# A rotation's sine product moved into the transposed-tile buffer, and VectorE's lane work placed behind the rotations already traced

## The chip, the core and the metric

The kernel runs on one NeuronCore of a Trainium2 chip. The metric is device time in microseconds (us) for one launch. PE is TensorE's matrix multiply, VectorE and ScalarE are the two elementwise engines, GpSimd a third one, and SP is the queue of SyncE, which issues nearly all transfers (DMAs) of this kernel. Each engine takes its own queue of instructions in order; semaphores make one wait for another.

## What is computed

One decoder layer over 2048 positions of width 1024 in fp32: adaptive RMS norm, one wide projection, two recurrent mixers side by side (HGRN2 and retention), their gated sum, an output projection, a last norm. The change lies in the retention half and in the order of the work beside it:

```python
proj = h @ w_in        # split: hq hf hi hz | rq rk rv rz | ga gb
qB = rotary(rq); kB = rotary(rk)          # per head: [t1*cos - t2*sin, t1*sin + t2*cos]
scores = einsum('bhnid,bhnjd->bhnij', qc, kc) * Dm
oB = scores @ vc + (qc * xi) @ R_prev     # R = gamma^C * R + (kc*zeta)^T vc, over chunks of 128
S_t = diag(f_t) S_{t-1} + (1 - f_t) i_t^T ; o_t = S_t^T q_t      # HGRN2
m = sigmoid(ga) * (norm(oA) * silu(hz)) + sigmoid(gb) * (norm(oB) * silu(rz))
out = rms_norm(x + gate * (m @ w_out))
```

## The kernel before

**Tiling.** The 2048 positions are two halves (`sb` 0 and 1) of eight chunks of 128 (`c`; chunk numbers run 0 to 15 in tile names). The eight heads are four pairs `p`. For each half and pair, `do_pair` runs four projections with weights streamed in from HBM: `a` (HGRN2's f and q, tiles gf and gq), `c` (values, gv), `b` (retention's q and k, gr; only for p = 0 and p = 2, each for two pairs) and `d` (the gates, gg, once per head). A projection of one chunk is 8 steps (`kt`) of 3 matmuls of 128x512: each fp32 operand is a high and a low fp32r part, and `mm3` adds hi*hi, hi*lo and lo*hi. Accumulators are PSUM tiles `pd`, three of them in rotation, so a projection's chunk can start when the chunk three before it has been read out.

**Weights.** `Ring` holds nine (hi, lo) weight tiles. When PE has used a tile for the last time (in the last chunk of a projection, step by step), `release` lets the next be split: ScalarE copies the high part (L468, wha to whd), VectorE subtracts for the low part (L469, wla to wld). The raw weights come by DMA on SP (L456).

**Rotations.** There are four groups of eight rotations, at (sb 0, p 0), (sb 0, p 2), (sb 1, p 0), (sb 1, p 2): the first, second, third and fourth group below. `rotate` reads one gr accumulator on VectorE: product with the cosine into `qk` (L754, two buffers), product with the sine into `qs` (L754, one buffer), a subtraction (L762) and an addition (L763) that make the turned q and k in `qk`, a 32x32 block transposition of `qk` into `tr` (L766, two buffers), and the zeta-weighted k into `kz` (L768, two buffers). Then `send` posts five DMAs on SP (L779, L783) that write `tr` and `kz` to DRAM. The accumulator is free when both products are done.

**Lanes.** Beside the projections run "lanes": `tree` (HGRN2's decay products), `hgrn_out` (HGRN2's outputs, tiles poh, and the states st) and `retention`. Each projection step ticks a counter in `Background`; every 9 ticks `burst` traces one more piece of each lane. For chunk 0 `hgrn_out` issues the poh matmuls on PE, a copy of the new state (st, L729) or its update (L731) on VectorE, then sums of squares on ScalarE (L681), a power on GpSimd (L115) and the scaling into v on VectorE (L684). In the second half the states are first scaled (L697). `retention` fetches turned k and q for a chunk by DMAs on SP (qpad L803, kpad L804, kT L807), then PE makes the scores (rt), VectorE weights them (scm, L824), and PE makes por.

**Order.** PE keeps program order. The other engines' queues are ordered by a scheduler from its own estimates of readiness, within the dependencies; buffers of a tag are reused in turn, and a write into a reused buffer waits for its last reader (for `tr`: the four DMAs that send it). `tc.issue_after(ins)` adds, to each instruction traced inside its block on the engine of `ins`, the edge that it stands behind `ins`. The last two chunks of a gr projection (6 and 7, or 14 and 15) are computed together, step by step (`group_two`), and the pair's lanes start just before them, so that PE's queue holds poh and the first rt among the steps of gr_6, gr_7 and the first gg.

Of the kernel before, what the change touches and what calls it, by code (L numbers as in the profile page):

```python
# [9 lines left out]
F32 = mybir.dt.float32  # L10
# [12 lines left out]
P = 128  # L23
# [18 lines left out]
def tile_hybrid(ctx: ExitStack, tc: tile.TileContext, a: dict, out: bass.AP):  # L42
    nc = tc.nc
    V, S, G = nc.vector, nc.scalar, nc.gpsimd

    class InOrder:

        def __init__(self):
            self.on = False
# [14 lines left out]
    upool = ctx.enter_context(tc.tile_pool(name="upool", bufs=1))  # L64
# [9 lines left out]
    def small_ps(name, tag):  # L74
        return pp.tile([P, 512], F32, name=name, tag=tag, bufs=small[tag])
# [100 lines left out]
    def ada_row(j):  # L176

        acc = upool.tile([P, 512], F32, name=f"acc{j}", tag="qk", bufs=2)
        bg_ = upool.tile([P, 512], F32, name=f"gate{j}", tag="tr", bufs=2)
        nc.sync.dma_start(out=bg_, in_=a["bgate"][:, j * 512 : (j + 1) * 512].broadcast_to([P, 512]))  # L180
        for k2 in range(KT // 2):
            w = wpool.tile([P, 2, 512], F32, name=f"wg{j}_{k2}", tag="raw", bufs=NRAW)
            nc.sync.dma_start(out=w, in_=a["w_gate"][j, 2 * k2 : 2 * k2 + 2].rearrange("k p n -> p k n"))
            for i in range(2):
                kt = 2 * k2 + i
                if kt == 0:
                    V.tensor_scalar(out=acc, in0=w[:, i, :], scalar1=sc[:, 0:1], scalar2=None, op0=ALU.mult)
                else:
                    V.scalar_tensor_tensor(
                        out=acc, in0=w[:, i, :], scalar=sc[:, kt : kt + 1], in1=acc, op0=ALU.mult, op1=ALU.add  # L190
                    )
            yield
        ps = small_ps(f"gps{j}", "sc")
        PE.matmul(out=ps, lhsT=ones, rhs=acc, start=True, stop=True)
        V.tensor_tensor(out=bg_, in0=ps, in1=bg_, op=ALU.add)
        gate[j] = bg_

    gate = {}
# [13 lines left out]
    for i in range(NQP):  # L212
        t = cpool.tile([P, 256], F32, name=f"qpad{i}", tag=f"qpad{i}")
# [5 lines left out]
    for i in range(NQP):  # L219
        t = cpool.tile([P, 256], F32, name=f"kpad{i}", tag=f"kpad{i}")  # L220
# [9 lines left out]
    class Background:  # L230

        def __init__(self):
            self.lanes = []
            self.side = []
            self.late = []
            self.since = 0.0
            self.beat = 0.0
            self.bursts = 0
            self.now = 0.0
            self.posts = []  # L240

        def burst(self):
            self.bursts += 1
            done, now = False, list(self.lanes)
            while now:
                again = []
                for g in now:
                    try:
                        said = next(g)
                    except StopIteration:  # L250
                        self.lanes.remove(g)
                        done = True
                        continue
                    done = done or said is not True
                    if said == "mid":
                        again.append(g)
                now = again
            self.merges()
            return done
# [48 lines left out]
    bg = Background()  # L308
# [27 lines left out]
    def x_rstd(t, xt, nm):  # L336
        sq = upool.tile([P, 512], F32, name=f"sq{nm}", tag="sg", bufs=3)
        ss = upool.tile([P, 2], F32, name=f"xss{nm}", tag="ss", bufs=4)
        for i in range(2):
            S.activation(out=sq, in_=xt[i], func=AF.Square, accum_out=ss[:, i : i + 1])  # L340
        r = upool.tile([P, 2], F32, name=f"xr{nm}", tag="rr", bufs=4)
        V.tensor_tensor(out=r[:, 0:1], in0=ss[:, 0:1], in1=ss[:, 1:2], op=ALU.add)
        rstd_of(r[:, 0:1], r[:, 0:1], 1, D)
        return r[:, 0:1]
# [38 lines left out]
    def block_r(b):  # L383

        rb = upool.tile([P, 512], F32, name=f"rb{b}", tag="qk", bufs=2)
        for t in range(4):
            xt = []
            for i in range(2):
                xt.append(upool.tile([P, 512], F32, name=f"xt{b}_{t}_{i}", tag="tr", bufs=2))
                nc.sync.dma_start(out=xt[i], in_=a["x"][(4 * b + t) * P : (4 * b + t + 1) * P, i * 512 : (i + 1) * 512])  # L390
            yield
            yield
            r = x_rstd(t, xt, f"b{b}_{t}")
            dg = upool.tile([P, P], F32, name=f"dgr{b}_{t}", tag="jk", bufs=1)
            G.tensor_scalar(out=dg, in0=ident, scalar1=r, scalar2=None, op0=ALU.mult)
            yield
            yield
            ps = small_ps(f"rb{b}_{t}", "sc")
            PE.matmul(out=ps[:, 0:P], lhsT=ones, rhs=dg, start=True, stop=True)
            S.activation(out=rb[:, t * P : (t + 1) * P], in_=ps[:, 0:P], func=AF.Copy)  # L400
        rbs[b] = rb
# [343 lines left out]
    turned_qk, rot = {}, {}  # L745

    def rotate(p, gc, ps):

        nm = f"{p}_{gc}"
        qk = upool.tile([P, 512], F32, name=f"qk{nm}", tag="qk", bufs=2)  # L750
        qs = upool.tile([P, 512], F32, name=f"qs{nm}", tag="qs", bufs=1)
        pv = ps.rearrange("p (g d) -> p g d", d=32)
        for dst, tab in ((qk, rot["cos"]), (qs, rot["sin"])):
            V.tensor_tensor(  # L754
                out=dst.rearrange("p (g d) -> p g d", d=32),
                in0=pv,
                in1=tab[:, gc % CH * 32 : (gc % CH + 1) * 32].unsqueeze(1).broadcast_to([P, 16, 32]),
                op=ALU.mult,
            )
        qkv = qk.rearrange("p (g two d) -> p g two d", two=2, d=32)  # L760
        qsv = qs.rearrange("p (g two d) -> p g two d", two=2, d=32)
        V.tensor_tensor(out=qkv[:, :, 0, :], in0=qkv[:, :, 0, :], in1=qsv[:, :, 1, :], op=ALU.subtract)  # L762
        V.tensor_tensor(out=qkv[:, :, 1, :], in0=qkv[:, :, 1, :], in1=qsv[:, :, 0, :], op=ALU.add)  # L763

        tr = upool.tile([P, 512], F32, name=f"tr{nm}", tag="tr", bufs=2)
        V.transpose(out=tr, in_=qk)  # L766
        kz = upool.tile([P, 256], F32, name=f"kz{nm}", tag="kz", bufs=2)
        V.tensor_tensor(  # L768
            out=kz.rearrange("p (w j d) -> p w j d", w=2, j=2),
            in0=qk.rearrange("p (w s j d) -> p w s j d", w=2, s=2, j=2)[:, :, 1],  # L770
            in1=zeta[:, 2 * p : 2 * p + 4].rearrange("p (w j) -> p w j", w=2).unsqueeze(3).broadcast_to([P, 2, 2, 64]),
            op=ALU.mult,
        )
        dm = dpool.tile([512, P], F32, name=f"qkT{nm}", tag="qkT", bufs=2 * CH)
        dz = dpool.tile([P, 256], F32, name=f"kz{nm}", tag="kzd", bufs=2 * CH)

        def send():
            for i in range(4):
                nc.sync.dma_start(  # L779
                    out=dm[:, 32 * i : 32 * i + 32].rearrange("(j a) t -> a j t", a=32),  # L780
                    in_=tr[32 * i : 32 * i + 32].rearrange("a (j t) -> a j t", t=32),
                )
            nc.sync.dma_start(out=dz, in_=kz)  # L783
            for w in range(2):
                turned_qk[p + w, gc] = (dm[256 * w : 256 * w + 256], dz[:, P * w : P * w + P])

        bg.post(4.0, send)
# [100 lines left out]
    def do_pair(sb, p, hook):  # L888
# [50 lines left out]
        if p % 2 == 0:  # L939
            for c, ps in group_toks(sb, ("b", sb, p), f"gr{p}", 0, start_lanes):  # L940
                rotate(p, sb * CH + c, ps)
# [157 lines left out]
    for j in range(2):  # L1099
        t = fgs[:, j * 512 : (j + 1) * 512]  # L1100
# [141 lines left out]
```

## Time and profile before

| | us |
|---|---|
| three runs: median (lowest to highest) | 2126.49 (2126.24 to 2127.15) |
| the profiled execution | 2124.74 |
| its span, first to last instruction | 2122.9 |
| PE busy, matmuls | 2053.1 |
| VectorE busy | 1097.3 |
| ScalarE busy | 572.3 |

The mean granted TensorE clock of the profiled execution is 0.989 of full speed. The page gives the busy time of each engine and the chain of work that ended last; the waits say for each instruction what ended the idle time before it; the timeline lists instructions by start and length; windows give busy times and the granted clock by stretch.

### The profile page before, as it was taken

Reading aid. Unit: us, or ns where it says so; the run is one execution under the profiler, and the core shown is the slowest. Engines: PE = TensorE matmul, PEld = TensorE weight load, DVE = VectorE, ACT = ScalarE, POOL = GpSimd, SP = SyncE. Lnnn points to the kernel's source line nnn. Section 1 sums busy time; section 2 is a strip of 40 time slices with the busy share of each in tenths; the row PEclk is TensorE's granted clock in tenths of the full one; section 3 lists DMA queues with packets and bytes.
Section 4 is the critical chain, followed back from the end, with each engine's and each line's share of the span. In section 5 each row is a group of like instructions: output and inputs, shape, how many; then the busy total and the mean of one; then the engine's idle time right before and its main releaser. Section 6 shows DMA issues by size and latency. Waiting matters only on the chain.

```text
span 2122.9 us, 38010 instructions
## 1 busy us (share of the span) xinstructions
PE 2053.1 (97%) x15320; PEld 1710.0 (81%) x15320; DVE 1097.3 (52%) x2441; ACT 572.3 (27%) x1389; POOL 139.8 (7%) x274
## 2 busy tenths in 40 slices
PE   6999999999997999999997999999997999999998
PEld 4887888888886888887886888888886888888886
DVE  7366544553455534557454544454454544567553
ACT  7212321332122221334221221332121221324221
POOL 1000100010001100121000100010000100010000
PEclk9999999999999999999999999999999999999999
DMA  8135221322144221434144221322144221346531
GB/s 310 41 74 128 63 65 41 91 60 57 41 103 107 78 55 41 105 109 141 41 103 94 69 63 41 84 65 58 41 103 105 70 61 41 84 142 191 175 133 60
DMA packets 322799, 187.65 MB, mean 88 GB/s; under 512 B 236096, under 2 KB 284736, under 8 KB 322624
## 3 DMA queue, kind: packets, MB, share of 16 engines
q1 hardware_dynamic: 322624, 185.23, 32.3%
q8 instruction: 120, 1.97, 0.4%
q14 instruction: 55, 0.45, 0.1%
HBM read 147.39 MB, written 37.75 MB: 87 GB/s over the span
## 4 chain that ended last, share of the span: by engine, by line
PE 91%; DVE 4%; DMA 2%; SPq 1%; issue 1%; POOL 1%; ACT 0%; DVEq 0%; POOLq 0%; ACTq 0%
PE gg L52 30%; PE gv L52 16%; PE gq L52 8%; PE ops L52 8%; PE gf L52 8%; PE gr L52 8%; PE poh L52 4%; PE por L52 4%; PE lv L52 3%; PE rt L52 1%; DVE wa L169 1%; DMA kT<-qkT 0%; DVE tr L766 0%; DMA k<-dk 0%; DVE h L358 0%
## 5 line engine op out<-in xcount | busy, mean ns | idle before, releaser
L52 PE MATMUL gg<-whd,h 128*128 128x512 f32 x2048 | 662.5, 396 | 4.6 <-DVE qs L754 4.6
L52 PEld LDWEIGHTS gg<-whd,h 128*128 128x128 f32 x2048 | 386.7, 189 | 84.7 <-issue 6.3
L52 PE MATMUL gg<-wld,h 128*128 128x512 f32 x1024 | 400.0, 391 | 1.5 <-DVE wld L469 1.5
L52 PE MATMUL gv<-whc,h 128*128 128x512 f32 x1024 | 331.5, 397 | 0.0
L52 PEld LDWEIGHTS gv<-whc,h 128*128 128x128 f32 x1024 | 193.1, 189 | 41.1 <-DVE h L358 0.4
L52 PEld LDWEIGHTS gg<-wld,h 128*128 128x128 f32 x1024 | 193.7, 189 | 39.4 <-DVE wld L469 1.9
L52 PE MATMUL gv<-wlc,h 128*128 128x512 f32 x512 | 199.2, 392 | 0.8 <-DVE wlc L469 0.8
L52 PE MATMUL gr<-whb,h 128*128 128x512 f32 x512 | 162.0, 392 | 0.0
L52 PE MATMUL gf<-h,wha 128*128 128x512 f32 x512 | 159.0, 390 | 2.1 <-DVE h L358 2.1
L52 PE MATMUL gq<-h,wha 128*128 128x512 f32 x512 | 157.7, 389 | 0.0
L52 PE MATMUL ops<-wo,mh 128*128 128x512 f32 x512 | 157.6, 389 | 0.0
L468 ACT ACTIVATE whd<-wd 128x512 fp32r<-128x512 f32 x128 | 78.1, 628 | 191.4 <-DMA wd<-in_w_d_dram 91.1
L612 DVE TENSOR_TENSOR q<-q,f 128x1024 f32<-128x1024 f32 x56 | 68.6, 1224 | 117.6 <-PE lv L52 117.6
L856 ACT ACTIVATE sgg<-gg 128x512 f32<-128x512 f32 x128 | 75.1, 596 | 172.9 <-PE gg L52 171.5
L469 DVE TENSOR_TENSOR wld<-wd,whd 128x512 fp32r<-128x512 f32 x128 | 85.7, 687 | 58.9 <-ACT whd L468 58.9
L52 PEld LDWEIGHTS gf<-h,wha 128*128 128x128 f32 x512 | 96.1, 188 | 24.1 <-DVE h L358 3.5
L115 POOL TENSOR_TENSOR rrr<-ssr,mhalf 128x2 f32<-128x2 f32 x64 | 44.8, 700 | 1039.7 <-DVE ssr L114 1039.7
L52 PEld LDWEIGHTS gv<-wlc,h 128*128 128x128 f32 x512 | 96.7, 189 | 20.4 <-DVE wlc L469 1.4
L52 PEld LDWEIGHTS gr<-whb,h 128*128 128x128 f32 x512 | 96.1, 188 | 20.0
L52 PEld LDWEIGHTS ops<-wo,mh 128*128 128x128 f32 x512 | 96.1, 188 | 20.0
L52 PEld LDWEIGHTS gq<-h,wha 128*128 128x128 f32 x512 | 96.0, 188 | 19.9
L681 ACT ACTIVATE jkr<-por 128x128 f32<-128x128 f32 x128 | 35.5, 277 | 242.6 <-DVE rs L843 201.8
(162 smaller groups left out, 2897.0 us busy)
## 6 DMA issues: line engine op xcount, KB each, us to landing
wd<-in_w_d_dram SPq DMA_DIRECT2D x64, 512.0 KB, 3.7
wc<-in_w_c_dram SPq DMA_DIRECT2D x32, 512.0 KB, 3.7
wa<-in_w_a_dram SPq DMA_DIRECT2D x32, 512.0 KB, 3.7
wa<-in_w_ada_dram SPq DMA_DIRECT2D x16, 512.0 KB, 8.3
wb<-in_w_b_dram SPq DMA_DIRECT2D x32, 256.0 KB, 3.2
qkT<-tr SPq DMA_DIRECT2D x128, 64.0 KB, 2.6
dk<-f SPq DMA_DIRECT2D x16, 512.0 KB, 2.8
k<-dk SPq DMA_DIRECT2D x64, 128.0 KB, 3.8
```

Of the source, the lines that this page charges most:

```text
L52: made = nc.tensor.matmul(**kw)
L115: G.tensor_tensor(out=dst, in0=ss, in1=mhalf.broadcast_to([P, width]), op=ALU.pow)
L169: V.tensor_tensor_reduce(out=w, in0=w, in1=scb, scale=1.0, scalar=bad[:, i * KT + kt : i * KT + kt + 1], op0=ALU.mult, op1=ALU.add, accum_ ...
L468: S.activation(out=hi, in_=w, func=AF.Copy)
L469: V.tensor_tensor(out=lo, in0=w, in1=hi, op=ALU.subtract)
L612: V.tensor_tensor(out=qv, in0=qv, in1=tv[:, :, :, 0:1].broadcast_to([P, NU, nb, m]), op=ALU.mult)
L681: S.activation(out=junk, in_=po[:, i * P : (i + 1) * P], func=AF.Square, accum_out=ss[:, i : i + 1])
L856: S.activation(out=sg, in_=ps, func=AF.Sigmoid)
```

## The change

`rotate` has no `qs` any more: the sine product is written into the `tr` buffer, from which subtraction and addition read it, and the transposition then overwrites it. `tr` has three buffers (also for the two other users of the tag, `ada_row` and `block_r`), `kz` has three. And `Background.burst` runs inside `issue_after` of the last rotation's kz product, so that VectorE's instructions of a burst stand behind the rotations that were traced before it.

```diff
+            self.hold = None
         def burst(self):
+            if self.hold is None:
+                return self.one_burst()
+            with tc.issue_after(self.hold):
+                return self.one_burst()
+        def one_burst(self):
...
-        qs = upool.tile([P, 512], F32, name=f"qs{nm}", tag="qs", bufs=1)
+        tr = upool.tile([P, 512], F32, name=f"tr{nm}", tag="tr", bufs=3)
         pv = ps.rearrange("p (g d) -> p g d", d=32)
-        for dst, tab in ((qk, rot["cos"]), (qs, rot["sin"])):
+        for dst, tab in ((qk, rot["cos"]), (tr, rot["sin"])):
...
-        qsv = qs.rearrange("p (g two d) -> p g two d", two=2, d=32)
+        qsv = tr.rearrange("p (g two d) -> p g two d", two=2, d=32)
...
-        tr = upool.tile([P, 512], F32, name=f"tr{nm}", tag="tr", bufs=2)
         V.transpose(out=tr, in_=qk)
-        kz = upool.tile([P, 256], F32, name=f"kz{nm}", tag="kz", bufs=2)
-        V.tensor_tensor(
+        kz = upool.tile([P, 256], F32, name=f"kz{nm}", tag="kz", bufs=3)
+        last = V.tensor_tensor(
             out=kz.rearrange("p (w j d) -> p w j d", w=2, j=2),
...
+        bg.hold = last.ins
```

In `ada_row` and `block_r` the diff only raises `bufs` of the tag `tr` from 2 to 3.

PE's queue holds the same rows in the same order as before. SP's queue differs only where `block_r` loads x between the halves, at a dozen of 765 rows, ScalarE's at 3 rows. What moves is VectorE's queue, in the four groups.

Second group (sb 0, p 2), VectorE before, from the last addition of rotation 4 on (the number behind the name is the chunk; st_129 and st_130 are the states of the two heads):

```order
L763 TENSOR_TENSOR qk_4_6085<-qk_4_6085,qs_4_6086 128x8x32
L729 COPY st_129<-poh_0_6151 128x128
L729 COPY st_130<-poh_0_6151 128x128
L469 TENSOR_TENSOR wld_6171<-wd_0_5778,whd_6170 128x512
L684 SCALAR_TENSOR_TENSOR v_0_5221<-poh_0_6151,rrh_0_6159,gn_2_0_6139 128x128 x2
L469 TENSOR_TENSOR wld_6183<-wd_1_5838,whd_6182 128x512
L469 TENSOR_TENSOR wld_6202<-wd_1_5838,whd_6201 128x512
L731 SCALAR_TENSOR_TENSOR st_129<-st_129,tl_0_5886,poh_1_6230 128x128
L731 SCALAR_TENSOR_TENSOR st_130<-st_130,tl_0_5886,poh_1_6230 128x128
L684 SCALAR_TENSOR_TENSOR v_1_5324<-poh_1_6230,rrh_1_6240,gn_2_0_6139 128x128 x2
L766 STREAM_TRANSPOSE tr_3_6049<-qk_3_6043 128x512
L768 TENSOR_TENSOR kz_3_6051<-qk_3_6043,zeta 128x256
```

The same place now, from the transposition of rotation 4 on:

```order
L773 STREAM_TRANSPOSE tr_4_6074<-qk_4_6073 128x512
L775 TENSOR_TENSOR kz_4_6080<-qk_4_6073,zeta 128x256
L477 TENSOR_TENSOR wld_6157<-wd_0_5770,whd_6156 128x512
L477 TENSOR_TENSOR wld_6169<-wd_1_5830,whd_6168 128x512
L477 TENSOR_TENSOR wld_6188<-wd_1_5830,whd_6187 128x512
L762 TENSOR_TENSOR tr_5_6115<-gr_5_6084,sin_1069 128x512
L770 TENSOR_TENSOR qk_5_6114<-qk_5_6114,tr_5_6115 128x8x32
L771 TENSOR_TENSOR qk_5_6114<-qk_5_6114,tr_5_6115 128x8x32
L773 STREAM_TRANSPOSE tr_5_6115<-qk_5_6114 128x512
L775 TENSOR_TENSOR kz_5_6121<-qk_5_6114,zeta 128x256
L737 COPY st_129<-poh_0_6137 128x128
L737 COPY st_130<-poh_0_6137 128x128
```

Behind it stand now st of poh_1, v_0, st, v_1, rotations 6 and 7, and only then the next two weight splits. Rotations 3, 4 and 5 have moved ahead of everything that hangs on poh_0 and poh_1; before, their transpositions stood behind both.

Third group (sb 1, p 0; the fourth group moves alike), VectorE before, behind rotation 12's additions:

```order
L469 TENSOR_TENSOR wld_10805<-wd_0_10422,whd_10804 128x512
L469 TENSOR_TENSOR wld_10817<-wd_1_10482,whd_10816 128x512
L469 TENSOR_TENSOR wld_10836<-wd_1_10482,whd_10835 128x512
L731 SCALAR_TENSOR_TENSOR st_125<-st_125,tl_1_10534,poh_8_10864 128x128
L731 SCALAR_TENSOR_TENSOR st_126<-st_126,tl_1_10534,poh_8_10864 128x128
L684 SCALAR_TENSOR_TENSOR v_8_9865<-poh_8_10864,rrh_8_10874,gn_0_0_10787 128x128 x2
L766 STREAM_TRANSPOSE tr_11_10697<-qk_11_10691 128x512
L768 TENSOR_TENSOR kz_11_10699<-qk_11_10691,zeta 128x256
```

The same place now:

```order
L477 TENSOR_TENSOR wld_10814<-wd_1_10466,whd_10813 128x512
L762 TENSOR_TENSOR tr_13_10755<-gr_13_10724,sin_10484 128x512
L770 TENSOR_TENSOR qk_13_10754<-qk_13_10754,tr_13_10755 128x8x32
L771 TENSOR_TENSOR qk_13_10754<-qk_13_10754,tr_13_10755 128x8x32
L773 STREAM_TRANSPOSE tr_13_10755<-qk_13_10754 128x512
L775 TENSOR_TENSOR kz_13_10761<-qk_13_10754,zeta 128x256
L705 TENSOR_SCALAR st_125<-st_125,f_1_9832 128x128
L705 TENSOR_SCALAR st_126<-st_126,f_1_9832 128x128
L739 SCALAR_TENSOR_TENSOR st_125<-st_125,tl_1_10518,poh_8_10842 128x128
L739 SCALAR_TENSOR_TENSOR st_126<-st_126,tl_1_10518,poh_8_10842 128x128
```

The two state scalings (L697 before, L705 now) stood some 90 rows earlier, in the a projection; they are now behind rotation 13.

Also in the third group, VectorE now, at rotations 11 to 13 (before, both products of a rotation stood together):

```order
L762 TENSOR_TENSOR qk_11_10672<-gr_11_10642,cos_10482 128x512
L762 TENSOR_TENSOR qk_12_10713<-gr_12_10683,cos_10482 128x512
L762 TENSOR_TENSOR tr_11_10673<-gr_11_10642,sin_10484 128x512
L770 TENSOR_TENSOR qk_11_10672<-qk_11_10672,tr_11_10673 128x8x32
L771 TENSOR_TENSOR qk_11_10672<-qk_11_10672,tr_11_10673 128x8x32
L773 STREAM_TRANSPOSE tr_11_10673<-qk_11_10672 128x512
L775 TENSOR_TENSOR kz_11_10679<-qk_11_10672,zeta 128x256
L762 TENSOR_TENSOR qk_13_10754<-gr_13_10724,cos_10482 128x512
L762 TENSOR_TENSOR tr_12_10714<-gr_12_10683,sin_10484 128x512
```

The sine product of a rotation stands behind the cosine product of the next one, which reads the next accumulator.

## Rows read from the trace of the kernel before

**Rows 1.** The page: busy time of engines (share), and the last chain by engine.

```profile
PE 2053.1 (97%) x15320; PEld 1710.0 (81%) x15320; DVE 1097.3 (52%) x2441; ACT 572.3 (27%) x1389; POOL 139.8 (7%) x274
...
PE 91%; DVE 4%; DMA 2%; SPq 1%; issue 1%; POOL 1%; ACT 0%; DVEq 0%; POOLq 0%; ACTq 0%
```

**Rows 2.** Waits of PE, whole span: who <- what ended it: us, times, longest.

```profile
PE rt L52 <- DMA kT<-qkT: 28.8, 3, 9.8
...
PE gg L52 <- DVE qs L754: 4.6, 3, 1.5
PE poh L52 <- DMA k<-dk: 4.1, 2, 3.7
PE rb L52 <- POOL dgr L395: 2.5, 2, 1.4
...
PE gg L52 <- DVE wld L469: 1.5, 1, 1.5
```

**Rows 3.** Timeline of VectorE, second group: start, length, instruction [idle before <- releaser].

```profile
623.36 0.69 DVE L754 TENSOR_TENSOR qk<-gr,cos 128x512 f32<-128x512 f32 x1 [3.35 <-PE gr L52]
...
628.80 0.69 DVE L754 TENSOR_TENSOR qk<-gr,cos 128x512 f32<-128x512 f32 x1 [2.42 <-PE gr L52]
...
635.81 0.49 DVE L729 COPY st<-poh 128x128 f32<-128x128 f32 x2 [4.93 <-PE poh L52]
...
639.41 1.28 DVE L469 TENSOR_TENSOR wld<-wd,whd 128x512 fp32r<-128x512 f32 x2
643.28 0.61 DVE L731 SCALAR_TENSOR_TENSOR st<-st,tl,poh 128x128 f32<-128x128 f32 x2 [2.59 <-PE poh L52]
645.86 0.61 DVE L684 SCALAR_TENSOR_TENSOR v<-poh,rrh,gn 128x128 f32<-128x128 f32 x2 [1.97 <-POOL rrh L115]
646.39 0.70 DVE L766 STREAM_TRANSPOSE tr<-qk 128x512 f32<-128x512 f32 x1
...
647.43 0.69 DVE L754 TENSOR_TENSOR qk<-gr,cos 128x512 f32<-128x512 f32 x1
648.04 0.68 DVE L754 TENSOR_TENSOR qs<-gr,sin 128x512 f32<-128x512 f32 x1
...
650.54 0.69 DVE L754 TENSOR_TENSOR qk<-gr,cos 128x512 f32<-128x512 f32 x1
```

**Rows 4.** Timeline of PE, second group.

```profile
642.19 0.39 PE L52 MATMUL poh<-st,q 128*128 128x128 f32 x2
...
660.93 1.22 PE L52 MATMUL rt<-qpad,kT 128*128 128x256 f32 x2 [9.78 <-DMA kT<-qkT]
```

**Rows 5.** Timeline of SP's queue, second group: rotation 5 is sent.

```profile
653.28 2.26 SPq L779 DMA_DIRECT2D qkT<-tr  x4
```

**Rows 6.** The last chain in order of time, second to fourth group: start, length, piece.

```profile
662.15 2.21 PE poh L52 x12
...
1143.10 1.19 PE rt L52 x2
1144.30 2.56 PE poh L52 x12
1146.86 7.00 PE gg L52 x27
1153.86 0.43 PE rt L52 x2
...
1155.63 1.34 PE poh L52 x12
...
1631.51 6.15 PE gg L52 x27
```

**Rows 7.** Windows: stretch, length, busy PE, PEld, DVE, ACT, POOL, granted clock, DMA, GB/s.

```profile
182.00:186.00 4.00, 3.65 (x16) 3.05 (x17) 3.97 (x9) 0.60 (x1) 0.00 (x0) 1.00 0.53 130
...
198.00:202.00 4.00, 4.00 (x14) 3.46 (x14) 0.49 (x2) 0.74 (x4) 0.74 (x2) 0.50 0.84 114
...
1143.00:1147.00 4.00, 3.90 (x15) 3.73 (x16) 1.79 (x4) 1.63 (x3) 0.00 (x0) 0.50 0.88 297
```

More of the change, by code (lines that the diff above doesn't have):

```diff
@@ L178, in ada_row @@
         acc = upool.tile([P, 512], F32, name=f"acc{j}", tag="qk", bufs=2)
-        bg_ = upool.tile([P, 512], F32, name=f"gate{j}", tag="tr", bufs=2)
+        bg_ = upool.tile([P, 512], F32, name=f"gate{j}", tag="tr", bufs=3)
         nc.sync.dma_start(out=bg_, in_=a["bgate"][:, j * 512 : (j + 1) * 512].broadcast_to([P, 512]))
@@ L388, in block_r @@
             for i in range(2):
-                xt.append(upool.tile([P, 512], F32, name=f"xt{b}_{t}_{i}", tag="tr", bufs=2))
+                xt.append(upool.tile([P, 512], F32, name=f"xt{b}_{t}_{i}", tag="tr", bufs=3))
                 nc.sync.dma_start(out=xt[i], in_=a["x"][(4 * b + t) * P : (4 * b + t + 1) * P, i * 512 : (i + 1) * 512])
```

## The prediction

> **What bounds the kernel now.** First the page: PE is busy 2053.1 of 2122.9 us and makes up 91% of the chain that ended last [rows 1]. So only PE's idle time, 69.8 us, is to be had, and what it loses to a lower clock behind idle stretches. The waits of PE say where that is [rows 2]. The largest is the score matmul rt, waiting three times for the DMA that brings kT, 28.8 us in all; close to each of the three stands a wait of gg for the sine product of a rotation, together 4.6 us. These are the second, third and fourth group of rotations. The timeline of VectorE in the second group shows the reason [rows 3]. Rotation 3's accumulator is ready at 623.36, but its transposition runs at 646.39. In between VectorE stands at the copy of a state, which waits 4.93 us for poh, then at the state's update (2.59 us) and at the normalisation behind it (1.97 us). All these are lane work, and rotations 3 to 7 are queued behind them. SP sends rotation 5 only at 653.28 [rows 5], the load of kT for the first rt is queued behind that send, and PE stands 9.78 us until 660.93 [rows 4]. Everything else is hidden: VectorE is busy 52%.
>
> **What is removed.** Waits: 28.8 + 4.6 = 33.4 us in three places [rows 2]. Then the clock. Behind the wait of the third group the granted clock is 0.50, the 1.2 GHz level [rows 7]: rt and the twelve poh matmuls take 1.19 + 2.56 = 3.75 us there, 0.43 + 1.34 = 1.77 us a little later at full clock; the 27 gg matmuls after them 7.00 against 6.15 [rows 6]. That is 1.98 + 0.85 = 2.83 us. In the second group it is 1.22 + 2.21 - 1.77 = 1.66 [rows 4, 6]. With the fourth taken like the third the sum is 33.4 + 1.66 + 2 x 2.83 = **40.7 us**, the most that the change can bring at these places.
>
> **What comes in its place, second group.** PE's order is the same, so I lay VectorE's new queue beside PE's old times.
> - An accumulator is complete every 5.44 us (623.36, 628.80 [rows 3]), so gr_5 at 634.24. A whole rotation takes 650.54 - 647.43 = 3.11 us [rows 3]. Rotation 4 now finishes its last four steps behind the cosine of rotation 5, at some 637.3. The accumulator of gr_4 is free 0.61 + 0.68 us after 634.24, at 635.5, just when PE comes to gr_7 behind gr_6's first step and poh_0: no wait, or 0.1 us.
> - The three weight splits that follow cannot be earlier than now, since they wait, through ScalarE, for PE to release tiles in gr_7: the last ended at 639.41 + 1.28 = 640.7 [rows 3]. Rotation 5's sine product and the rest, 2.5 us, are done at 643.1, its transposition at 642.6.
> - Only now come the state copies. They began at 635.81 [rows 3]; the first ends at 643.25. PE's matmul on the copied state stood at 642.19 [rows 4] and **waits 1.05 us**.
> - The load of kT: from the send of rotation 5 to the start of rt took 660.93 - 653.28 = 7.65 us [rows 4, 5], so kT is there at 642.6 + 7.65 = 650.3. PE came to rt at 660.93 - 9.78 = 651.15; less the 1.5 us that gg waits no more, plus 1.05, that is 650.7. The wait for kT is gone, by a margin of only 0.4 us.
> - Next is late: the next weight splits. VectorE has to do the state update, two normalisations, each 1.97 us behind its state [rows 3], and rotations 6 and 7. The copies end at 643.5, v_0 is made from 645.4 to 646.0, v_1 from 648.3 to 648.9, the two rotations last to 655.1, the first split to 655.75. PE comes to that tile after rt, poh_2 and four more matmuls (6.15 / 27 = 0.23 us each [rows 6]): 650.7 + 1.77 + 0.9 = 653.4. It **waits 2.4 us**, and some 0.25 us more for the two splits behind the score weighting.
>
> New waits in the second group: 1.05 + 2.4 + 0.25 = **3.7 us**.
>
> **Third and fourth group.** Two things differ. PE has no poh between gr_14 and gr_15, so gr_15 waits for gr_12's sine product: that ends 1.29 us after gr_13 is complete, PE has 0.7 us of gr_14 to do and comes there a little before VectorE sees gr_13: **0.85 us**. This delays the releases and with them the three splits and rotation 13. The state scalings behind it hold the state matmul of poh_8, about **1.0 us** more. Only one normalisation stands ahead of the last two rotations, so the split wait is smaller, **1.2 + 0.25 us**. Together 3.3 us each, by the same durations.
>
> **The rest at nothing.** The sine product is the same instruction with another target, 32 times, so no work is added. In the first group VectorE has work at every moment and only the score weighting slips behind rotation 7's last two steps, some 1 us; PE's next long wait there is for k (3.7 us [rows 2]), whose chain does not pass through it. Without that cover it would cost that 1 us. The earlier x loads between the halves touch PE only at its waits for rb, 2.5 us in all [rows 2]: between a gain of 2.5 and a loss of the same, since SP takes these loads ahead of others; I take 0, as the second load of each pair, which ends the wait, keeps its place.
>
> **Sum.** 40.7 - 3.7 - 2 x 3.3 = 30.4 us. The profiled execution took 2124.74 us, 1.75 us under the median of 2126.49; taken off the median, 30.4 gives **2096 us**.
>
> **The clock.** Not every wait lowers it. After the wait of 1.5 us for a weight split the granted clock stayed at 1.00; behind the one of 3.7 us for k it was 0.50 [rows 2, 7]. The new waits, of 0.85 to 2.4 us, lie between, nearer to the first, so I add nothing in the forecast. The Trainium skill ("TensorE: Matmul & The Clock Gate", "What's actually happening") says that the gate follows recent activity on a phase of its own that does not start with the program; by that a wait of such a length may lower the clock in one place and not in the next. The rows agree as far as they go. By the row the sum stays at 30.4; by the rule up to the old loss returns in each place.
>
> **Rivals.**
> - The clock falls at the new waits too. For it speaks that each place has two or three of them within some 15 us; against it that the old 1.5 us waits of gg did nothing by themselves. Price: at most 2.83 us in each of three places, 8.5: 2104.6 us.
> - kT stays last. SP's order is unchanged there and the margin is 0.4 us. What speaks against it: a late kT of up to 2.4 us only takes the place of the split wait. Were the send 5 us late, three places would cost some 2.6 us each: 2104 us.
> - The new waits are smaller than worked out, because ScalarE or the ends of instructions run ahead of my durations. Half of the 10.3 us: 2091 us; none of them: 2086.
> - It does not do what it says: the queue moves but rt waits as before for something else ahead of kT on SP: 2126 us. The one candidate, the send of rotation 5, moves 10 us earlier, so this is unlikely.
> - Slower: rotation 5's sine product must wait until the DMAs that send rotation 2 have landed, as must rotation 13's for rotation 10. PE's state matmul now stands behind it. If these sends were held on SP until late, each us of it would be a us of PE's. They come out ahead only if it is under 13 us a place, 40.7 / 3; at 15 us the time is 2131 us. Rotation 2 is turned 16 us before, and SP is not blocked then, so a small chance.
>
> **How the numbers follow.** Forecast with small changes of its terms, 2091 to 2101: 0.62. Clock: 0.17. kT late: 0.08. Smaller waits: 0.07. No change: 0.03. Slower: 0.03. Keeping out some 0.15, the range is 2088 to 2107. Faster by over 0.2% (4.3 us, about what a measurement of this kernel can tell from no change): 0.94; within: 0.03; slower: 0.03.
>
> **What would show it.** In the trace of the changed kernel rt no longer waits for kT, or under 1 us each; gg no longer waits for a rotation; instead poh waits about 1 us for the state's copy or scaling, and gg 1 to 2.5 us for wld, in three places; in the second half gr waits 0.85 us for the sine product. The transposition of rotation 5 in the second group stands near 642.6. A new kT wait of several us, or a clock of 0.50 in these stretches, would make the forecast too low; no wait for wld, too high.

## The result

The changed kernel takes 2099.18 us (median of four runs, 2098.8 to 2100.86), the kernel before 2126.36 us on the same chip: a ratio of 0.9875, 95% interval 0.9858 to 0.9892. That is 27.2 us less; 30.4 were forecast, and 2096 us with a range of 2088 to 2107. Run again beside the experiments below, the changed kernel took 2097.24 us, ratio 0.9866 (0.9851 to 0.9881).

The page of the changed kernel, its busy line and the chain by engine, answers [rows 1]. The span is 2097.1 us instead of 2122.9. PE is busy for 2.2 us less, so 23.6 of the 25.8 us are idle time that is gone:

```profile
PE 2050.9 (98%) x15320; PEld 1706.1 (81%) x15320; DVE 1096.1 (52%) x2441; ACT 570.8 (27%) x1389; POOL 139.7 (7%) x274
...
PE 88%; DVE 6%; DMA 3%; issue 1%; ACT 1%; POOL 1%; SPq 1%; DVEq 0%; POOLq 0%; ACTq 0%
```

The waits of PE in the changed kernel (who <- what ended it: us in total, times, longest) answer [rows 2]:

```profile
PE gg L52 <- DVE wld L477: 6.2, 4, 2.2
...
PE poh L52 <- DMA k<-dk: 4.7, 2, 4.0
...
PE poh L52 <- DVE st L705: 1.9, 2, 0.9
...
PE gr L52 <- DVE tr L762: 1.6, 2, 0.8
...
PE poh L52 <- DVE st L737: 0.9, 1, 0.9
...
PE rt L52 <- DMA kT<-qkT: 0.8, 1, 0.8
```

The three kT waits of 9.4 to 9.8 us and gg's waits for a rotation are gone. In their place stand the short ones that the prediction named: a weight split (four, one of which stood before), a state copy or scaling, a sine product. A single kT wait of 0.8 us is new and was not forecast.

VectorE in the second group, changed kernel (start, length, instruction, in brackets the idle time before it and its releaser), to be held against [rows 3]:

```profile
633.88 0.69 DVE L762 TENSOR_TENSOR qk<-gr,cos 128x512 f32<-128x512 f32 x1 [2.30 <-PE gr L52]
...
636.00 0.71 DVE L773 STREAM_TRANSPOSE tr<-qk 128x512 f32<-128x512 f32 x1
...
640.32 0.69 DVE L762 TENSOR_TENSOR tr<-gr,sin 128x512 f32<-128x512 f32 x1
...
641.83 0.71 DVE L773 STREAM_TRANSPOSE tr<-qk 128x512 f32<-128x512 f32 x1
...
642.77 0.48 DVE L737 COPY st<-poh 128x128 f32<-128x128 f32 x2
```

Rotation 4's transposition (636.00) and rotation 5's (641.83) stand ahead of the state copies now; before, rotation 3's came at 646.39 [rows 3]. SP follows: rotation 5 is sent at 642.57, not at 653.28 [rows 5], and the load of kT issues 4.35 us later:

```profile
642.57 1.95 SPq L787 DMA_DIRECT2D qkT<-tr  x4
...
646.92 0.47 SPq L815 DMA_DIRECT2D kT<-qkT  x1
```

To see where the gain came from, take the first cosine product of the second, third and fourth group as marks. Timeline of VectorE, the kernel before:

```profile
608.54 0.65 DVE L754 TENSOR_TENSOR qk<-gr,cos 128x512 f32<-128x512 f32 x1
...
1091.80 0.65 DVE L754 TENSOR_TENSOR qk<-gr,cos 128x512 f32<-128x512 f32 x1
...
1566.53 0.65 DVE L754 TENSOR_TENSOR qk<-gr,cos 128x512 f32<-128x512 f32 x1
```

The changed kernel:

```profile
608.18 0.65 DVE L762 TENSOR_TENSOR qk<-gr,cos 128x512 f32<-128x512 f32 x1
...
1084.91 0.65 DVE L762 TENSOR_TENSOR qk<-gr,cos 128x512 f32<-128x512 f32 x1
...
1549.63 0.65 DVE L762 TENSOR_TENSOR qk<-gr,cos 128x512 f32<-128x512 f32 x1
```

| stretch | before | after | gained | forecast |
|---|---|---|---|---|
| start to second group | 608.54 | 608.18 | 0.4 | 0 |
| second to third group | 483.26 | 476.73 | 6.5 | 9.3 |
| third to fourth group | 474.73 | 464.72 | 10.0 | 10.7 |
| fourth group to the end of the span | 556.37 | 547.47 | 8.9 | 10.4 |
| sum | 2122.9 | 2097.1 | 25.8 | 30.4 |

So the mechanism holds in each of the three places, and 4.6 us of the forecast are missing in the profiled executions, more than half of them in the stretch of the second group.

### The profile page after: what moved, and what is told of

Its sections match the earlier page's. It is cut to its first block, busy times and chain, and to the rows that moved or that the text cites. A ratio compares the mean times of both kernels' runs of the same rounds, so it can differ in the third digit from the quotient of the medians.

```text
span 2097.1 us, 37999 instructions
## 1 busy us (share of the span) xinstructions
PE 2050.9 (98%) x15320; PEld 1706.1 (81%) x15320; DVE 1096.1 (52%) x2441; ACT 570.8 (27%) x1389; POOL 139.7 (7%) x274
## 4 chain that ended last, share of the span: by engine, by line
PE 88%; DVE 6%; DMA 3%; issue 1%; ACT 1%; POOL 1%; SPq 1%; DVEq 0%; POOLq 0%; ACTq 0%
PE gg L52 30%; PE gv L52 16%; PE gq L52 8%; PE ops L52 8%; PE gf L52 8%; PE gr L52 6%; PE por L52 4%; PE poh L52 3%; PE lv L52 3%; PE rt L52 1%; DVE wld L477 1%; DMA wd<-in_w_d_dram 1%; DVE wa L169 1%; DVE tr L762 0%; DMA k<-dk 0%
```

## The experiments

The runs ask three things. Which part of the change moves the rotations: the hold, or the buffers? What are the new waits worth, and can they be had back? And what does the clock add? Each kernel was timed against runs of the kernel before on the same chip; ratios are to those. By the short names in the headings, e0, e1, e2 and e4 ran on one chip, e7, e8 and e10 on a second, e12 and e14 on a third, and the last pair on a fourth.

**The changed kernel once more (e0).**

> The changed kernel once more, for a second profile of it. Waits of PE should repeat to 0.1 us (they hang on lengths of instructions). Theory: the granted clock is not tied to a wait; it fell behind the 2.16 us wait for a weight split of the second group and in the stretch between the halves, but not behind waits of the same kind in the third and fourth groups, so in this profile the stretches at 0.50 may lie elsewhere; time 2099 us, within 3 us. Rival: the clock falls behind each wait over 2 us, so it falls again at exactly the same two places.

It took 2097.24 us. The waits in the last three groups repeat: 0.94 (state copy) and 2.15 us (split) in the second group, 0.79, 0.93 and 1.33 in the third, 0.80, 0.93, 1.33 and 0.71 (kT) in the fourth. The clock repeats in one place and not in the other. Windows of the first profile of the changed kernel (stretch, length, busy PE, PEld, DVE, ACT, POOL, granted clock, DMA, GB/s):

```profile
654.00:656.00 2.00, 0.74 (x3) 0.62 (x4) 2.00 (x5) 0.00 (x0) 0.00 (x0) 1.00 0.00 0
656.00:658.00 2.00, 2.00 (x6) 1.51 (x6) 1.60 (x4) 0.00 (x0) 0.00 (x0) 0.56 0.57 150
...
982.00:984.00 2.00, 1.81 (x4) 0.58 (x3) 0.80 (x3) 0.17 (x2) 0.93 (x3) 0.50 0.75 205
```

The same two places in the second profile, where all lies 1.4 to 2 us earlier:

```profile
654.00:656.00 2.00, 2.00 (x6) 1.51 (x6) 2.00 (x5) 0.00 (x0) 0.00 (x0) 0.50 0.14 47
...
980.00:982.00 2.00, 1.14 (x3) 0.39 (x3) 0.92 (x4) 0.67 (x3) 0.81 (x3) 1.00 0.75 222
```

Behind the split wait of the second group the clock is 0.50 both times. Between the halves it is 0.50 in one execution of the same program and 1.00 in the other. Second to third group took 1081.87 - 606.69 = 475.18 us in the second profile, 1.55 less than the 476.73 of the first. About 1.2 of it lies between the halves: from the rb matmul ahead of the fall (970.92 and 969.05) to the third group it is 113.99 us in the first profile and 112.82 in the second. Another 0.5 is no matter of the clock: poh waits 0.70 us there for the DMA of k in the first profile and 0.23 at the same row in the second. Theory and rival each get one place right; e4 and e7 below speak against the rival. The Trainium skill ("TensorE: Matmul & The Clock Gate", "What's actually happening") says that the gate's phase does not start with the program; the place between the halves agrees with it.

**The hold alone (e1).** The kernel before, with these lines added:

```diff
+            if self.hold is None:
+                return self.one_burst()
+            with tc.issue_after(self.hold):
+                return self.one_burst()
...
+        bg.hold = last.ins
```

> The kernel before plus the hold alone: the lanes' instructions on VectorE stand behind the last rotation traced, but the sine product keeps its own single buffer, and there are two buffers each of transposed tiles and zeta-weighted k. Theory (the hold does it): nearly the whole gain, 2099 to 2103 us, no kT wait. Rival (the buffers do it): VectorE's order then puts three weight splits and the transposition of rotation 3 ahead of rotation 5, whose transposition must wait for the send of rotation 3; the state's copy or scaling comes some 4.9 us late for PE in each of the last three groups and the clock may fall there (1.7 to 2.8 us a place): 2102 to 2111 us, with poh waiting for st about 5 us three times, kT under 1 us.

It took 2105.16 us, ratio 0.9899 (0.9882 to 0.9915). Waits of PE in it:

```profile
PE poh L52 <- DVE st L704: 7.4, 2, 3.7
...
PE poh L52 <- DVE st L736: 3.7, 1, 3.7
```

The hold does take the kT waits away, but VectorE's order then puts three splits, the transpositions of rotations 3 and 4 and all of rotation 5 ahead of the state, and poh waits 3.7 us for it in each of the last three groups. Behind each of these waits the granted clock falls (0.50 at 645 to 647 and at 1121 to 1125 us, 0.56 at 1592 to 1594). That is the rival's picture, with 3.7 us where 4.9 was expected; the hold alone gives some 20 of the 27 to 28 us.

**The buffers alone (e2).** The changed kernel less one line:

```diff
-        bg.hold = last.ins
```

> The changed kernel without the hold: sine product in the transposed-tile buffer, three buffers of transposed tiles and of zeta-weighted k, lanes not held. Theory (the hold does it): rotations 3 to 7 are again behind lane work, kT waits of over 5 us return in each group, 2115 to 2126 us. Rival (the buffers do it): in the third and fourth group VectorE's order is that of the changed kernel but without the state scalings behind rotation 13, so poh no longer waits 0.93 us there, twice; in the second group the state's copy and one normalisation stand ahead of rotation 4's sine product, gr_7 waits some 3.4 us for it, the split wait falls to about 1 us: 2097 to 2102 us, no kT wait over 1 us.

It took 2097.37 us, ratio 0.9864 (0.9849 to 0.9878): as fast as the changed kernel (2097.24 beside it). Its waits:

```profile
PE gr L52 <- DVE tr L762: 5.4, 3, 3.8
...
PE rt L52 <- DMA kT<-qkT: 0.5, 2, 0.3
```

So in the changed kernel the hold is worth nothing that the intervals can tell. VectorE without it in the second group shows what it does:

```profile
634.51 0.69 DVE L762 TENSOR_TENSOR qk<-gr,cos 128x512 f32<-128x512 f32 x1 [2.30 <-PE gr L52]
636.08 0.49 DVE L737 COPY st<-poh 128x128 f32<-128x128 f32 x2 [0.88 <-PE poh L52]
638.53 0.61 DVE L692 SCALAR_TENSOR_TENSOR v<-poh,rrh,gn 128x128 f32<-128x128 f32 x2 [1.97 <-POOL rrh L115]
639.06 0.68 DVE L762 TENSOR_TENSOR tr<-gr,sin 128x512 f32<-128x512 f32 x1
```

Without the hold the copy and a normalisation stand ahead of rotation 4's sine product, and gr_7 waits 3.85 us for the accumulator; the split wait behind is 1.33. Together 5.2 us, against 0.94 + 2.16 = 3.1 in the changed kernel. In the third and fourth group the state scaling is not held, and 0.93 us of poh's wait each time does not arise. The two, 2.1 us against 1.9, cancel.

**The product in place, nothing else (e12).** As the last, with the third buffers taken back (in `ada_row` and `block_r` too):

```diff
-        tr = upool.tile([P, 512], F32, name=f"tr{nm}", tag="tr", bufs=3)
+        tr = upool.tile([P, 512], F32, name=f"tr{nm}", tag="tr", bufs=2)
...
-        kz = upool.tile([P, 256], F32, name=f"kz{nm}", tag="kz", bufs=3)
+        kz = upool.tile([P, 256], F32, name=f"kz{nm}", tag="kz", bufs=2)
```

> One part of the change alone: the sine product goes into the buffer of its transposed tile (no buffer of its own), but there stay two buffers each of transposed tiles and of zeta-weighted k, and nothing is held. Theory (the in-place product itself is what moves the rotations): the transposition now has to follow its own products, so VectorE's queue has rotations 3 to 5 as in e2_buffers_only; the sends of rotations two before have landed long before they are waited for; no kT wait over 1 us, one wait of gr for rotation 4's sine product of some 3.9 us, 2096 to 2099 us. Rival (the third buffers are needed): the sine product waits for the send two rotations before, PE waits for gr in every group, several us each: over 2105 us.

It took 2099.26 us, ratio 0.9869 (0.9853 to 0.9886), with gr waiting 3.85 us in the second group and one kT wait of 1.4:

```profile
PE gr L52 <- DVE tr L762: 5.4, 3, 3.8
...
PE rt L52 <- DMA kT<-qkT: 1.4, 1, 1.4
```

The single edit of writing the sine product where the transposed tile will lie therefore carries the gain, to within what the intervals resolve. In the kernel before, a rotation's products ran ahead into a buffer of their own, and its transposition was put off behind lane work. With the product in place each transposition of the last three groups follows its own additions, with one exception: in the second group rotation 5's additions end at 647.76, and its transposition stands behind a state update that waits for poh:

```profile
649.07 0.35 DVE L739 SCALAR_TENSOR_TENSOR st<-st,tl,poh 128x128 f32<-128x128 f32 x1 [1.31 <-PE poh L52]
649.33 0.70 DVE L773 STREAM_TRANSPOSE tr<-qk 128x512 f32<-128x512 f32 x1
```

That is the group with the kT wait of 1.4 us; with the third buffers (e2) it follows at once, at 647.98, and PE does not wait for kT in that group. So the product in place does not force the order, it changes what the scheduler chooses; why it chooses so, no run shows. The third buffers with the product in a buffer of its own were not run.

**The hold without the state scalings (e4).**

```diff
+        def held(self):
+            return tc.issue_after(self.hold) if self.hold is not None else ExitStack()
...
-                normed(po, v, 0, f"h{p}_{gc}", gn)
+                with bg.held():
+                    normed(po, v, 0, f"h{p}_{gc}", gn)
```

and the same around the state's copy or update; `burst` holds nothing more.

> The changed kernel, but only the state's copy or update and the normalisation of HGRN2 are held behind the rotations; the state scalings of the second half, the retention lane and the decay products are free. Theory: poh's wait for the scaling (0.93 us in the third and fourth group) goes, and what follows moves up with it: 1.9 us less, 2097.3 us. Rival: the next wait, for the weight split (1.33 us) or kT (0.76 us), grows by the same, and the time stays at 2099 us.

2095.05 us, ratio 0.9853 (0.9839 to 0.9868), 2.2 us under the changed kernel beside it. Poh's wait for L705 is gone, and the split waits did not grow (1.20 and 1.16, from 1.33). The intervals overlap; the waits carry the reading. In the profile the clock also stayed at 1.00 behind the split wait of the second group, where it fell in the changed kernel, so a part of the 2.2 us may be the clock.

**Rotations in order (e7).** On top of that, each rotation behind the last instruction of the one before:

```diff
+        with tc.issue_after(turn[0]) if turn[0] is not None else ExitStack():
+            tr, kz = turned(p, gc, ps)
```

> The kernel of e4_hold_no_scale with one more edge on VectorE: each rotation's instructions stand behind the last instruction of the rotation before, so that a cosine product no longer runs ahead of the sine product of the rotation before. Theory: the 0.80 us that gr_15 waits for rotation 12's sine product, in the third and fourth group, goes, and all that follows moves up by as much: 1.6 us under e4 (2095.05 us), so 2093.5 us. Rival: the wait for the weight split behind it (1.2 us) hangs on something else, grows by 0.8 us in each place, and the time stays at 2095 us.

2092.74 us, ratio 0.9841 (0.9827 to 0.9854); the four runs spread from 2090.73 to 2094.70, and the interval overlaps that of the kernel it is built on, so again the waits carry the reading. No wait of gr is left; the split waits are 2.26, 1.37 and 1.26. Of the 1.6 us some 0.4 came back there.

These two kernels also answer the question on the clock. The split wait of the second group is 2.14 us in e4 and 2.26 us here, and behind neither does the clock fall. The wait and the window behind it, e4 and then e7:

```profile
655.44 0.50 PE L52 MATMUL gg<-wld,h 128*128 128x512 f32 x1 [2.14 <-DVE wld L474]
655.00:659.00 4.00, 3.56 (x15) 2.73 (x16) 2.78 (x6) 0.00 (x0) 0.00 (x0) 1.00 0.48 137
...
655.20 0.50 PE L52 MATMUL gg<-wld,h 128*128 128x512 f32 x1 [2.26 <-DVE wld L474]
655.00:659.00 4.00, 3.81 (x16) 2.89 (x17) 2.53 (x6) 0.00 (x0) 0.00 (x0) 1.00 0.48 142
```

In both profiles of the changed kernel it fell behind 2.16 and 2.15 us in the same place. The rival of e0, a fall behind each wait over 2 us, is refuted.

The same rotations in order, in the kernel without the hold (e8):

```diff
-        bg.hold = last.ins
...
+        with tc.issue_after(turn[0]) if turn[0] is not None else ExitStack():
+            tr, kz = turned(p, gc, ps)
```

> The kernel of e2_buffers_only (no hold) with the rotations ordered as in e7. It differs from e7 in the second group alone: there the state's copy and a normalisation stand ahead of rotation 4's sine product. Theory (the hold is worth only what it does in the second group): gr_7 still waits about 3.85 us for that sine product, against poh 0.94 plus a split wait 0.8 us longer in e7, so it is 2 us above e7: 2095.5 us. Rival (the hold is worth nothing): equal to e7 within 1 us.

2096.91 us, ratio 0.9861 (0.9848 to 0.9875), 4.2 above e7. By its waits it is 3.85 + 1.45 against 0.94 + 2.26 in the second group, 2.1 us; in the profile the clock of this kernel was also 0.50 at 637 to 641 and at 982 to 990 us, where that of e7 was 1.00. The first of the two stands at the 3.85 us wait, the second between the halves, where it came and went in one and the same kernel. So the hold is worth some 2 us by the waits in the one place where the state's copy would come first; how much of the rest of the 4.2 belongs to it is open.

**Splits ahead of the last two rotations (e10).** In the changed kernel ScalarE has the high parts of two splits ready by 648.0 us, while VectorE first does rotations 6 and 7 and splits at 654.53:

```profile
646.84 1.14 ACT L476 ACTIVATE whd<-wd 128x512 fp32r<-128x512 f32 x2
```

The edit, on top of e7:

```diff
+        if gc % CH < CH - 1 or p + gc < CH:
+            bg.hold = last.ins
...
+            if gc % CH < CH - 2 or p + gc < CH:
+                tr, kz = turned(p, gc, ps)
+            else:
+                with tc.issue_after(ring.splits[-4 if gc % CH == CH - 2 else -2]):
+                    tr, kz = turned(p, gc, ps)
```

> The kernel of e7 with the last two rotations of the second, third and fourth group put behind weight splits on VectorE (rotation 6 or 14 behind the two splits of the third raw weight tile, rotation 7 or 15 behind the next two), and lane work held only up to rotation 6 or 14. Theory: the split waits (2.14, 1.20 and 1.16 us in e4) are caused by the two rotations ahead of the splits, whose high parts ScalarE had made over 6 us earlier; they go, 4.5 us, and the clock has less reason to fall in the second group: 4.5 to 6 us under e7, 2087.5 to 2089 us. Rival: VectorE has too much work in that stretch and the wait only moves, to the next split, to an accumulator that rotation 7 frees late, or to a state: under 2 us gained, 2091.5 us or above.

2086.64 us, ratio 0.9812 (0.9798 to 0.9825): 6.1 under e7. The split waits of the three groups are gone; 0.93 for the state's copy is the only wait left in these groups (the 0.5 for a split stands in the first group, where it was 1.4):

```profile
PE poh L52 <- DVE st L737: 0.9, 1, 0.9
...
PE gg L52 <- DVE wld L475: 0.5, 1, 0.5
```

**Rotation 5 ahead of the splits (e14).** On top of e10, in `pump`:

```diff
+                with tc.issue_after(bg.hold) if bg.hold is not None else ExitStack():
+                    self.split = V.tensor_tensor(out=lo, in0=w, in1=hi, op=ALU.subtract).ins
```

> The kernel of e10_split_first with one more edge: the weight splits stand behind the last rotation traced, so that rotation 5 or 13 is finished ahead of the three splits and the state's copies with it. Theory: poh's wait of 0.93 us for the state's copy in the second group goes, kT comes some 4 us earlier, no other wait takes its place: 1 us under e10 (2086.64 us), 2085.7 us. Rival: the splits, 1 to 3 us later now, become late for gg: 2086.6 us or above with a wait for wld of 0.5 us or more.

2081.92 us, ratio 0.9788 (0.9773 to 0.9802). No wait of PE is left in the last three groups of rotations; that of the state's copy is gone and no split is late; the one row for a split stands in the first group:

```profile
PE gg L52 <- DVE wld L476: 0.5, 1, 0.5
```

The step down was 4.7 us where one wait of 0.93 was to be had, so both kernels ran once more, side by side.

> The kernel of e10_split_first once more, beside e14 on one chip. Between the two, PE's waits differ by 0.93 us alone, but the medians by 4.7 us (2086.64 and 2081.92, each against its own runs of before, 2126.17 and 2127.38). Theory: the rest is where the granted clock happened to be 0.50 (13 to 24 us and 979 to 983 us in the profile of e10, neither in that of e14), and will not repeat: 1 to 3 us between the two here. Rival: the rest belongs to the order: 4 us or more again.

> The kernel of e14_turn_first once more, beside e10_again. Theory: 1 to 3 us below it, 2082 to 2085 us. Rival: 4 us or more below it.

e10 again took 2085.68 us, ratio 0.9807 (0.9794 to 0.9820), and e14 again 2083.65 us, ratio 0.9798 (0.9785 to 0.9811): 2.0 us apart, with the same waits as before but for the one. The rest of the 4.7 did not repeat. The clock's part in it is likely, not shown: the first pair differed in two stretches at 0.50 (13 to 24 and 979 to 983 us, in the slower kernel alone), the second in none (neither has the first, both have the second). This last kernel is 2.0 to 2.1% faster than the kernel before (both its runs), the changed kernel 1.3%.

## Why the prediction was right, and where its sizes were off

**The bound and the mechanism: right.** rt no longer waits in any of the three places, rotation 5's send moved from 653.28 [rows 5] to 642.57, and its transposition, put at 642.6, ended at 641.83 + 0.71 = 642.54. PE came to rt at 650.24 without a kT wait, against the 650.7 worked out. The feared wait of rotation 5's sine product for the send of rotation 2 did not show: it began right behind the split at 640.32.

**The new waits: right to within 0.3 us each.** Timeline of PE, changed kernel, the three places:

```profile
643.10 0.49 PE L52 MATMUL poh<-st,q 128*128 128x128 f32 x2 [0.94 <-DVE st L737]
...
655.26 0.50 PE L52 MATMUL gg<-wld,h 128*128 128x512 f32 x1 [2.16 <-DVE wld L477]
...
1112.05 0.47 PE L52 MATMUL gr<-whb,h 128*128 128x512 f32 x1 [0.79 <-DVE tr L762]
...
1119.84 0.49 PE L52 MATMUL poh<-st,q 128*128 128x128 f32 x2 [0.93 <-DVE st L705]
...
1131.17 0.50 PE L52 MATMUL gg<-wld,h 128*128 128x512 f32 x1 [1.33 <-DVE wld L477]
...
1602.35 0.67 PE L52 MATMUL rt<-qpad,kT 128*128 128x256 f32 x2 [0.76 <-DMA kT<-qkT]
```

1.05 was forecast for the first and 2.4 for the second, 0.85, 1.0 and 1.2 for the next three. The further 0.25 us in each place, for the two splits behind the score weighting, did not show. e4, e7, e10 and e14 then took the waits out one after the other, and the time followed each time.

**The clock: the term that was set at nothing.** "The clock" added nothing, from the row of a 1.5 us wait [rows 7]. That is the step that failed: the new waits lay between a wait of 1.5 us, after which the clock stayed, and one of 3.7, after which it was 0.50, and I took them all to be like the first. The clock fell behind the 2.16 us wait of the second group and not behind those of the third and fourth. Nor does the length decide it, as the step assumed: behind 2.14 us (e4) and 2.26 us (e7) in the same place the clock stayed. What does, no run here shows. The rival in which the clock falls at the new waits came true in one place of three. In the chain of the changed kernel 23 gg matmuls take 7.14 us behind that wait and 5.72 behind the 1.33 us wait of the third group, where the clock stayed:

```profile
655.26 7.14 PE gg L52 x23
...
1131.17 5.72 PE gg L52 x23
```

That is 1.4 us. The 1.2 us between the halves, of which no step spoke, come on top (in the kernel before the clock is 1.00 there), and 0.2 for a wait for k that was 0.48 us before and is 0.70 now; the waits of the second group came out 0.6 us shorter than forecast. 1.4 + 1.2 + 0.2 - 0.6 makes some 2.2 of the 2.7 us that the second stretch lacks.

**kT in the fourth group: not foreseen.** The margin of kT was worked out for the first rt alone. The second rt of the fourth group waited 0.76 us; in the chain its transfer takes 3.62 us from issue to landing, against 2.36 and 2.55 for the first rt of the third and second group in the kernel before. It was 0.71 in the second profile, 0.23 in e2 and is absent in e4, so it hangs on small shifts there.

```profile
1598.60 3.62 DMA kT<-qkT
```

With it the fourth stretch still lacks some 0.8 us, and the third 0.65, though its listed waits (3.05) are under the 3.3 of the forecast. No listed wait shows that remainder.

**What the clock gives back: taken too large.** The remainder lies in PE's busy time. Windows of the third and fourth stretch, the kernel before, then the changed kernel:

```profile
1091.80:1566.53 474.73, 463.52 (x3618) 388.68 (x3617) 230.28 (x526) 116.11 (x288) 25.38 (x48) 0.99 0.28 69
1566.53:2122.90 556.37, 535.75 (x3230) 447.61 (x3228) 288.97 (x627) 136.22 (x347) 37.78 (x80) 0.99 0.39 107
...
1084.91:1549.63 464.72, 461.56 (x3618) 386.44 (x3617) 229.83 (x525) 115.66 (x288) 25.47 (x48) 1.00 0.28 71
1549.63:2097.10 547.47, 533.97 (x3230) 445.32 (x3228) 289.17 (x629) 135.92 (x347) 37.93 (x80) 1.00 0.39 109
```

PE's idle time falls by 8.05 and 7.12 us, as the listed waits say (11.1 less 3.05 and 10.9 less 3.8). Its busy time had to fall by the 2.83 us put down to the clock in each place; it falls by 1.96 and 1.78 (2.23 and 1.63 in the second profile). A part of the difference is that a wait costs PE more than its listed idle time. Across the 0.79 us wait of the third group, from 1110.87 to 1112.36, it is 1.49 us, and 0.46 for the same rows before (1117.75 to 1118.21): 1.03 lost. Each place has three or four new waits for two old ones. How much of the rest is the clock is not separated.

**What the prediction did not separate.** It costed VectorE's new queue as a whole and said nothing of which edit makes it. The runs do: the product in place alone gives the gain (e12), the hold alone most of it with a new wait of 3.7 us (e1), and both together no more than the buffers alone (e2 beside e0). Undoing the hold would have lost nothing that the intervals can tell; that could have been read from the order of the changed kernel without it.

## What to carry to other kernels

An intermediate buffer of its own lets the first half of a chain run ahead on an in-order engine, and the second half, the one that others wait for, may then be queued behind a blocked instruction. Here writing the intermediate into the buffer of the result kept nearly all these chains together, at no cost in space; look at the queue's order to see whether it does elsewhere. And when a wait of 10 us is gone, the next ones are worth a look: here nine more, of 0.8 to 2.2 us and 10 us by their listed times, went with four further edits of one engine's order, and the time fell by another 14 to 15 us (2097.24 to 2083.65 and 2081.92, on different chips).

## What the hardware showed that was not expected

The same program had a granted clock of 0.50 at 982 to 986 us in one profiled execution and 1.00 there in another, with PE's waits in that stretch no longer than 1.41 us in either; the stretch was about 1.2 us longer with the fall.

The length of a wait does not settle whether the clock falls behind it. At the split wait of the second group it fell behind 2.16 and 2.15 us in both profiles of the changed kernel, and stayed behind 2.14 us (e4) and 2.26 us (e7). Behind the waits of 3.7 to 3.9 us in the groups of rotations (three in e1, one each in e2, e8 and e12) it fell each time; but of the thirteen profiles here, each with a wait of 3.4 to 4.5 us for xt near 13 us, only five have the clock at 0.50 behind it.
